# Spacing out the side work of the experts' stages in a two-block transformer forward pass

## The chip, the cores and the metric

The kernel runs on one core of a Trainium2 chip. The metric is the device time of one execution in microseconds, the median of several runs. Five engines work side by side: TensorE (PE, its weight loads shown as PEld), VectorE (DVE), ScalarE (ACT), GpSimd (POOL) and SyncE (SP), which here only issues DMAs. Each takes its instructions in the order in which the program wrote them.

## What is computed

256 positions of width 2048 go through two blocks in float32. The first has four attention mixers and an MLP; the second has a retention and a recurrent branch, a cross-attention, and a layer of 16384 single-neuron experts, which the change is about:

```python
def peer_ffn(xn, w_q, sub_keys, u_tab, v_tab):
    q = (xt @ w_q).reshape(t, PEER_HEADS, 2, PEER_HALF)
    sub_scores = jnp.einsum('thcd,hckd->thck', q, sub_keys).astype(jnp.float32)
    vals, ids = lax.top_k(sub_scores, PEER_TOPK)
    cand = vals[:, :, 0, :, None] + vals[:, :, 1, None, :]
    top_sc, pos = lax.top_k(cand.reshape(t, PEER_HEADS, PEER_TOPK * PEER_TOPK), PEER_TOPK)
    i1 = jnp.take_along_axis(ids[:, :, 0], pos // PEER_TOPK, axis=-1)
    i2 = jnp.take_along_axis(ids[:, :, 1], pos % PEER_TOPK, axis=-1)
    gate = jax.nn.softmax(top_sc, axis=-1)
    ...
    act = jax.nn.gelu(jnp.einsum('td,tkd->tk', xb, u))
    return jnp.einsum('tk,tkd->td', gb * act, v_tab[eb])
```

For each position and head the 16 best of 16384 experts are selected. The kernel computes the activations of all experts, makes a dense matrix G of gates that is zero where an expert wasn't selected, and multiplies W = G x activation with the whole table v.

## The kernel before, in words

**One stream of weights.** Class Stream (line 43) holds all large matrix products of the program in one list. A piece is 1 MB of weights (128 x 2048 floats); it is loaded on SyncE's queue into a tile raw (three of them, load, line 69) and used in two half pieces of 128 x 1024. Each half piece is split into a rounded part whi (ScalarE copy, line 84) and the rest wlo (a subtraction, line 87), so that three products with rounded operands give float32 accuracy. There are five whi and five wlo tiles. Method run (line 139) goes through the half pieces in order: at half piece i it writes the split of half piece i+3 (ahead, line 90), then the products of half piece i, then the "end" of the output if this was its last half piece, and then some steps of the side work.

**Two modes.** In mode "w" the weights stand still and a half piece is 8 pairs of a 512-column product (line 173) and a 256-column product (line 174). In mode "t" the activations stand still and a half piece is 12 products of 512 columns (lines 163 to 165). Sums are in two PSUM tiles called mm, taken in turn.

**Side work** is a list of Python generators. Method steps (line 118) goes through the list once in each half piece and lets each generator write its instructions up to its next yield. A plain yield counts against the half piece's budget; "pause" and "wait" do not. The budget is 2 steps in the stage w_q and in the stage v, and 1 in the stage u (rate=1, line 1440). With even=True it is also 1, and the end of a generator doesn't count either. Nothing else sets the order: it is fixed when the program is built.

**The experts' stages** (peer, line 1390) are three runs of the stream:
- w_q, 32 half pieces, mode w: the queries. Every second half piece's wlo is made on GpSimd here (pool=2, lines 86 and 1408). Side work: normed (line 1464) scales the layer's input, two GpSimd operations for each of eight tiles fx, to give the tiles fn; topk (line 1498), once for each of four quarters of the heads, selects with top16 (line 1478: MAX8, MAX_INDEX and MATCH_REPLACE on VectorE, four rows each) and looks the numbers up with tiles eq, compared on VectorE (line 1555) and multiplied on GpSimd (line 1557).
- u, 256 half pieces, mode w: the activations, an output every four half pieces. gelu_pair (line 1445) works on each in three rounds of a ScalarE and a VectorE operation, directly in the PSUM tile, and stores the result (ad). Side work: the rest of topk, then gates (line 1564), 64 rounds with "yield" and "pause" in turn, which write G to memory (gd).
- v, 256 half pieces, mode t, 16 groups of 16. Four tiles W for each group come from weigh (line 1613): two products wx<-A,G on VectorE, a rounded copy on ScalarE (line 1635), a subtraction on VectorE (line 1636). weigh for a group runs while the group ahead of it is multiplied, after A and G came by DMA. At each output's end v_end (line 1419) adds the sums to the residual h (VectorE, line 1423, the profile's acc<-mm,acc).

After the last group finish (line 1643) does the final norm and stores the output.

The lines on which the order turns:

```python
            if j.get("even"):
                s.steps(1, ("wait", "pause", "end"))
            else:
                s.steps(j.get("rate", 2))
```

## Time and profile before

| what | value |
|---|---|
| median of 3 runs | 3544.64 us (3544.45 to 3547.34) |
| profiled execution, its own time | 3546.58 us |
| its span, first to last instruction | 3544.5 us |
| PE busy | 3483.2 us (98%) |
| PEld busy | 2957.8 us (83%) |
| DVE busy | 2306.4 us (65%) |
| ACT busy | 1636.6 us (46%) |
| POOL busy | 324.3 us (9%) |
| mean granted TensorE clock | 0.995 of full speed |
| moved by DMA | 703.84 MB, 199 GB/s |

The profile was taken on one execution. Busy is the time in which an engine had an instruction running; products overlap, each being shown at about 390 ns while the next one starts 227 ns after it, so a short wait of TensorE shows up smaller in its busy time than it is. The granted clock is 1 at full speed (2.4 GHz) and 0.5 at the lower level (1.2 GHz); for a stretch it is given as a mean.

### The profile page before, as it was taken

Reading aid. Unit: us, or ns where it says so; the run is one execution under the profiler, and the core shown is the slowest. Engines: PE = TensorE matmul, PEld = TensorE weight load, DVE = VectorE, ACT = ScalarE, POOL = GpSimd, SP = SyncE. Lnnn points to the kernel's source line nnn. Section 1 sums busy time; section 2 is a strip of 40 time slices with the busy share of each in tenths; the row PEclk is TensorE's granted clock in tenths of the full one; section 3 lists DMA queues with packets and bytes.
Section 4 is the critical chain, followed back from the end, with each engine's and each line's share of the span. In section 5 each row is a group of like instructions: output and inputs, shape, how many; then the busy total and the mean of one; then the engine's idle time right before and its main releaser. Section 6 shows DMA issues by size and latency. Waiting matters only on the chain.

```text
span 3544.5 us, 45984 instructions
## 1 busy us (share of the span) xinstructions
PE 3483.2 (98%) x18204; PEld 2957.8 (83%) x18204; DVE 2306.4 (65%) x3412; ACT 1636.6 (46%) x2298; POOL 324.3 (9%) x342
## 2 busy tenths in 40 slices
PE   9999999999999999999999899999999999999998
PEld 7788888888888888888888788888888888888887
DVE  5565565645555567875555998777776566766665
ACT  5455444444343454545444344555554444444443
POOL 0000000000000000010003522222220000000000
PEclk9999999999999999999999999999999999999999
DMA  6544455555555555445544455666666576666654
GB/s 217 173 143 164 176 184 179 200 183 196 181 197 197 206 185 196 155 157 197 204 156 169 148 196 206 220 231 208 232 220 251 201 270 235 237 237 237 238 208 154
DMA packets 112567, 703.84 MB, mean 199 GB/s; under 512 B 12708, under 2 KB 13493, under 8 KB 39392
## 3 DMA queue, kind: packets, MB, share of 16 engines
q1 hardware_dynamic: 87120, 610.98, 48.2%
q0 software_dynamic: 24944, 89.85, 7.3%
q8 instruction: 143, 2.34, 0.3%
q14 instruction: 72, 0.59, 0.0%
q10 hardware_dynamic: 288, 0.07, 0.0%
HBM read 660.98 MB, written 39.87 MB: 198 GB/s over the span
## 4 chain that ended last, share of the span: by engine, by line
PE 80%; DVE 10%; issue 6%; ACT 3%; POOL 1%; DMA 1%; ACTq 0%; POOLq 0%; SPq 0%; DVEq 0%
PE mm L173 26%; PE mm L174 13%; PE mm L164 11%; PE mm L163 11%; PE mm L165 11%; DVE wlo L87 4%; ACT whi L84 2%; DVE wx L1632 2%; PE ss L1602 2%; PE ss L318 1%; PE ss L266 1%; PE ss L345 1%; DVE eq L1555 0%; PE ss L1381 0%; PE ss L1359 0%
## 5 line engine op out<-in xcount | busy, mean ns | idle before, releaser
L87 DVE TENSOR_TENSOR wlo<-raw,whi 128x1024 fp32r<-128x1024 f32 (+2 forms) x1146 | 1394.8, 1240 | 460.2 <-ACT whi L84 458.6
L84 ACT ACTIVATE whi<-raw 128x1024 fp32r<-128x1024 f32 (+2 forms) x1162 | 1187.2, 1049 | 451.9 <-PE mm L165 330.1
L173 PE MATMUL mm<-xT,whi 128*128 128x512 f32 x2368 | 847.7, 401 | 0.0
L173 PE MATMUL mm<-fn,whi 128*128 128x512 f32 x2048 | 731.9, 401 | 3.6 <-ACT whi L84 2.6
L174 PE MATMUL mm<-xT,wlo 128*128 128x256 f32 x2368 | 666.2, 281 | 9.3 <-DVE wlo L87 9.1
L174 PE MATMUL mm<-fn,wlo 128*128 128x256 f32 x2048 | 576.5, 281 | 10.1 <-DVE wlo L87 10.1
L173 PEld LDWEIGHTS mm<-xT,whi 128*128 128x128 f32 x2368 | 446.6, 189 | 107.4 <-issue 1.6
L173 PEld LDWEIGHTS mm<-fn,whi 128*128 128x128 f32 x2048 | 387.8, 189 | 93.2 <-ACT whi L84 2.9
L174 PEld LDWEIGHTS mm<-xT,wlo 128*128 128x128 f32 x2368 | 449.1, 190 | 13.1 <-DVE wlo L87 12.3
L164 PE MATMUL mm<-wlo,W 128*128 128x512 f32 x1024 | 400.3, 391 | 12.2 <-DVE wlo L87 12.2
L174 PEld LDWEIGHTS mm<-fn,wlo 128*128 128x128 f32 x2048 | 390.1, 190 | 12.5 <-DVE wlo L87 12.5
L163 PE MATMUL mm<-whi,W 128*128 128x512 f32 x1024 | 399.5, 390 | 0.0
L165 PE MATMUL mm<-whi,W 128*128 128x512 f32 x1024 | 398.5, 389 | 0.0
L164 PEld LDWEIGHTS mm<-wlo,W 128*128 128x128 f32 x1024 | 192.2, 188 | 56.6 <-DVE wlo L87 17.2
L163 PEld LDWEIGHTS mm<-whi,W 128*128 128x128 f32 x1024 | 192.2, 188 | 43.2 <-ACT whi L84 3.4
L165 PEld LDWEIGHTS mm<-whi,W 128*128 128x128 f32 x1024 | 192.2, 188 | 39.5
L163 PE MATMUL mm<-whi,hid 128*128 128x512 f32 x512 | 199.8, 390 | 0.0
L165 PE MATMUL mm<-whi,hid 128*128 128x512 f32 x512 | 199.3, 389 | 0.0
L164 PE MATMUL mm<-wlo,hid 128*128 128x512 f32 x512 | 199.3, 389 | 0.0
L1423 DVE TENSOR_TENSOR acc<-mm,acc 128x512 f32<-128x512 f32 x128 | 82.2, 683 | 104.6 <-PE mm L165 104.6
L1452 DVE TENSOR_TENSOR mm<-mm,act 128x512 f32<-128x512 f32 x64 | 44.7, 698 | 153.3 <-ACT act L1451 153.3
L1451 ACT ACTIVATE act<-mm 128x512 f32<-128x512 f32 x64 | 38.2, 597 | 228.6 <-PE mm L174 228.6
(507 smaller groups left out, 4166.8 us busy)
## 6 DMA issues: line engine op xcount, KB each, us to landing
raw<-in_peer_u SPq DMA_DIRECT2D x128, 1024.0 KB, 5.0
raw<-in_peer_v SPq DMA_DIRECT2D x128, 1024.0 KB, 5.0
raw<-in_w_up SPq DMA_DIRECT2D x64, 1024.0 KB, 5.1
raw<-in_w_down SPq DMA_DIRECT2D x64, 1024.0 KB, 4.9
raw<-in_w_in_w SPq DMA_DIRECT2D x52, 1024.0 KB, 4.9
raw<-in_w_out SPq DMA_DIRECT2D x32, 1024.0 KB, 5.0
raw<-in_w_in_t SPq DMA_DIRECT2D x22, 1024.0 KB, 4.8
raw<-in_w_xv SPq DMA_DIRECT2D x16, 1024.0 KB, 4.9
```

Source lines behind the costliest of these rows:

```text
L84: s.nc.scalar.activation(hi[:, :w], raw, AF.Copy)
L87: e.tensor_tensor(lo[:, :w], raw, hi[:, :w].bitcast(F32), op=ALU.subtract)
L163: nc.tensor.matmul(o, xh, w, start=st, stop=False, skip_group_check=True)
L164: nc.tensor.matmul(o, xh, v, start=False, stop=False, skip_group_check=True)
L165: nc.tensor.matmul(o, xl, w, start=False, stop=en, skip_group_check=True)
L173: nc.tensor.matmul(o, w[:, c], xt[:, :, kl], start=st, stop=False, skip_group_check=True)
L174: nc.tensor.matmul(o[:, 0], v[:, c], xt[:, 0, kl], start=False, stop=en, skip_group_check=True)
L1423: nc.vector.tensor_tensor(h[:, m], acc[m], h[:, m], op=ALU.add)
L1451: nc.scalar.activation(a, z, AF.Copy)
L1452: nc.vector.tensor_tensor(y, y, a, op=ALU.add)
L1602: nc.tensor.matmul(p[:, j * 128:(j + 1) * 128], o[0][:, j], o[1][:, j], start=True, stop=True)
L1632: nc.vector.tensor_tensor(x[:, :, 128 * i:128 * i + 128], a[:, 2 * (e % 2):2 * (e % 2) + 2, 128 * i:128 * i + 128], G[s][i].rearrange("p ( ...
```

## The change

- **steps** knows a new word: a generator that yields "rest" ends the side work of this half piece, also for those behind it in the list.
- **Budgets**: w_q, u and v all get even=True, so one counting step in each half piece.
- **Selection and gates**: topk, top16 and gates yield "rest" after most of their steps, so such a step is written only in every second half piece; normed too.
- **No GpSimd** for the wlo of w_q, for fx in normed and for the product on eq in topk: all are VectorE's now. GpSimd keeps the product on oh in gates, a conversion in topk, and its DMAs.
- **gelu_pair** begins a half piece later and works on a tile ux in SBUF in place of the PSUM tile.
- **v_end** writes the additions a half piece later, except for the last output.
- **weigh** makes W in three stages over six half pieces: in one half piece the products of tile e, the rounded copy of tile e-1 and the subtraction of tile e-2. After the first load of A and G it lets four half pieces go by.

```diff
@@ Stream.steps
-            n -= s.step(g) not in idle
+            r = s.step(g)
+            if r == "rest":
+                return
+            n -= r not in idle
@@ peer: w_q, v_end, v, u
-                  pool=2,
+                  even=True,
...
         def v_end(s, n):
-            def end(acc):
+            def add(acc):
+                if (s, n) != (15, 3):
+                    yield "pause"
                 h = self.h[n]
                 for m in range(2):
                     nc.vector.tensor_tensor(h[:, m], acc[m], h[:, m], op=ALU.add)
+                if s == 15:
+                    S.side.append(self.finish(n))
+
+            def end(acc):
+                S.spawn(add(acc), first=True)
                 if n == 3:
                     have.add(f"v{s}")
-                if s == 15:
-                    S.side.append(self.finish(n))
...
-                      end=v_end(s, n))
+                      end=v_end(s, n), even=True)
...
-                  end=u_end(u), need=lambda kbs: kbs[-1] // 2 in self.fn, rate=1,
+                  end=u_end(u), need=lambda kbs: kbs[-1] // 2 in self.fn, even=True,
@@ gelu_pair
-        a = self.half_act[c][:, 2 * u:2 * u + 2]
+        a, x = self.half_act[c][:, 2 * u:2 * u + 2], self.w([128, 2, 256], "ux")
+        yield "pause"
         nc.scalar.activation(a, z, AF.Copy)
-        nc.vector.tensor_tensor(y, y, a, op=ALU.add)
+        nc.vector.tensor_tensor(x, y, a, op=ALU.add)
...
@@ normed
-            nc.gpsimd.tensor_tensor(x, t[:, 0].bitcast(F32), t[:, 1].bitcast(F32), op=ALU.add)
-            nc.gpsimd.tensor_tensor(x, x, self.Rf[:, None, :].to_broadcast([128, 2, 256]), op=ALU.mult)
-            yield "pause"
+            nc.vector.tensor_tensor(x, t[:, 0].bitcast(F32), t[:, 1].bitcast(F32), op=ALU.add)
+            nc.vector.tensor_tensor(x, x, self.Rf[:, None, :].to_broadcast([128, 2, 256]), op=ALU.mult)
+            yield "rest"
@@ top16
             if i:
                 yield
+                yield "rest"
             for v, idx, s in rows:
                 nc.vector.max_index(idx[:, c], v[:, c], s)
             yield
+            yield "rest"
@@ topk
         nc.vector.tensor_tensor(b, qs[:, 2], t[:, 0], op=ALU.subtract)
         yield
+        yield "rest"
...
-                    nc.gpsimd.tensor_tensor(eq[m][:, h], eq[m][:, h],
+                    nc.vector.tensor_tensor(eq[m][:, h], eq[m][:, h],
@@ gates
             yield
-            yield "pause"
+            yield "rest"
@@ weigh
         load(0)
+        for _ in range(4):
+            yield "pause"
         for s in range(16):
...
-            for e in range(4):
-                t, x = self.xe("W"), self.w([128, 2, 256], "wx")
...
-                nc.scalar.activation(t[:, 0], x, AF.Copy)
-                nc.vector.tensor_sub(t[:, 1], x, t[:, 0].bitcast(F32))
-                self.W[s, e] = t
+            W, X = {}, {}
+            for e in range(6):
+                if e > 1:
+                    nc.vector.tensor_sub(W[e - 2][:, 1], X[e - 2], W[e - 2][:, 0].bitcast(F32))
+                    self.W[s, e - 2] = W[e - 2]
+                if 0 < e < 5:
+                    W[e - 1] = self.xe("W")
+                    nc.scalar.activation(W[e - 1][:, 0], X[e - 1], AF.Copy)
+                if e < 4:
+                    X[e] = x = self.w([128, 2, 256], "wx")
...
                 yield
+            del G[s], A[s]
```

How it moves the instructions, at three places of VectorE's order. Rows with L87 are the splits, one for each half piece; what stands between two of them is what one half piece's side work adds (the line numbers of the change are up to 20 higher).

**First place: the selection, in w_q before.** tv and cv are the values found, ti and ci their places, sub and cand what is searched.

```order
L87 TENSOR_TENSOR wlo<-raw,whi 128x1024
L1485 MAX tv<-sub 128x8 x4
L1489 MAX_INDEX ti<-tv,sub 128x8 x4
L1474 TENSOR_TENSOR fn<-fx,fn 128x512
L1493 MATCH_REPLACE sub<-tv,sub 128x128 x4
L1485 MAX tv<-sub 128x8 x4
L87 TENSOR_TENSOR wlo<-raw,whi 128x1024
L1489 MAX_INDEX ti<-tv,sub 128x8 x4
L405 SCALAR_TENSOR_TENSOR pq<-mm,pq 128x512
L1474 TENSOR_TENSOR fn<-fx,fn 128x512
```

The same kind of steps with the change (a later quarter, in u; ux and act belong to gelu_pair):

```order
L1494 MAX cv<-cand 128x8 x4
L1499 MAX_INDEX ci<-cv,cand 128x8 x4
L87 TENSOR_TENSOR wlo<-raw,whi 128x1024 x2
L1461 TENSOR_TENSOR ux<-mm,act 128x512
L1504 MATCH_REPLACE cand<-cv,cand 128x64 x4
L1494 MAX cv<-cand 128x8 x4
L87 TENSOR_TENSOR wlo<-raw,whi 128x1024
L1464 SCALAR_TENSOR_TENSOR act<-act,ux 128x512
L87 TENSOR_TENSOR wlo<-raw,whi 128x1024
L1467 SCALAR_TENSOR_TENSOR act<-act,ux 128x512
L1499 MAX_INDEX ci<-cv,cand 128x8 x4
L87 TENSOR_TENSOR wlo<-raw,whi 128x1024 x2
```

Before, the steps of two generators and those of normed stand between two splits, and every second split is missing from this engine; with the change each split is here, and a step of the selection is followed by a half piece without one.

**Second place: the end of the selection**, before:

```order
L87 TENSOR_TENSOR wlo<-raw,whi 128x1024
L1555 TENSOR_TENSOR eq<-qs,cst 128x256 x4
L1561 TENSOR_REDUCE i_129<-eq 128x32 x2
L1555 TENSOR_TENSOR eq<-qs,cst 128x256 x4
L1485 MAX tv<-sub 128x8 x4
L1489 MAX_INDEX ti<-tv,sub 128x8 x4
L87 TENSOR_TENSOR wlo<-raw,whi 128x1024
```

and with the change (L1569 is the product that was GpSimd's):

```order
L87 TENSOR_TENSOR wlo<-raw,whi 128x1024
L1567 TENSOR_TENSOR eq<-qs,cst 128x256
L1569 TENSOR_TENSOR eq<-eq,tf 128x256
L1567 TENSOR_TENSOR eq<-qs,cst 128x256
L1569 TENSOR_TENSOR eq<-eq,tf 128x256
L1567 TENSOR_TENSOR eq<-qs,cst 128x256
L1569 TENSOR_TENSOR eq<-eq,tf 128x256
L1567 TENSOR_TENSOR eq<-qs,cst 128x256
L1569 TENSOR_TENSOR eq<-eq,tf 128x256
L87 TENSOR_TENSOR wlo<-raw,whi 128x1024
L1461 TENSOR_TENSOR ux<-mm,act 128x512
L1573 TENSOR_REDUCE i_129<-eq 128x32 x2
```

Four comparisons became four comparisons and four products; the next such group stands in the half piece right behind.

**Third place: a group's W in the stage v**, before:

```order
L1423 TENSOR_TENSOR acc<-mm,acc 128x512 x2
L1632 TENSOR_TENSOR wx<-A,G 128x2x128 x2
L1636 TENSOR_TENSOR W<-wx,W 128x512
L87 TENSOR_TENSOR wlo<-raw,whi 128x1024
L1632 TENSOR_TENSOR wx<-A,G 128x2x128 x2
L1636 TENSOR_TENSOR W<-wx,W 128x512
L87 TENSOR_TENSOR wlo<-raw,whi 128x1024
L1632 TENSOR_TENSOR wx<-A,G 128x2x128 x2
L1636 TENSOR_TENSOR W<-wx,W 128x512
L87 TENSOR_TENSOR wlo<-raw,whi 128x1024
L1632 TENSOR_TENSOR wx<-A,G 128x2x128 x2
```

and with the change:

```order
L1654 TENSOR_TENSOR wx<-A,G 128x2x128 x2
L87 TENSOR_TENSOR wlo<-raw,whi 128x1024
L1428 TENSOR_TENSOR acc<-mm,acc 128x512 x2
L1654 TENSOR_TENSOR wx<-A,G 128x2x128 x2
L87 TENSOR_TENSOR wlo<-raw,whi 128x1024
L1645 TENSOR_TENSOR W<-wx,W 128x512
L1654 TENSOR_TENSOR wx<-A,G 128x2x128 x2
L87 TENSOR_TENSOR wlo<-raw,whi 128x1024
L1645 TENSOR_TENSOR W<-wx,W 128x512
L1654 TENSOR_TENSOR wx<-A,G 128x2x128 x2
L87 TENSOR_TENSOR wlo<-raw,whi 128x1024
L1645 TENSOR_TENSOR W<-wx,W 128x512
```

Before, each subtraction into W stands right behind its own products; with the change it stands two half pieces behind them, and there is one tile's work in a half piece. In the whole order the last comparison for gates stands at VectorE's split 864 of 1162 (before at 839 of 1146, with 16 more splits on GpSimd, so at half piece 9 earlier), and the first half piece of v is that of split 910.

## Rows read from the trace of the kernel before

**Rows 1.** Busy time by stretch: start:end, length, PE, PEld, DVE, ACT, POOL, PEclk, DMA, GB/s.

```profile
1900.00:2150.00 250.00, 232.60 (x1288) 200.46 (x1287) 216.99 (x643) 106.98 (x140) 109.97 (x78) 0.97 0.50 177
...
2650.00:2750.00 100.00, 95.92 (x536) 82.69 (x536) 62.84 (x72) 48.56 (x67) 10.84 (x16) 0.97 0.68 244
...
2818.00:3532.00 714.00, 701.84 (x3071) 574.76 (x3070) 491.67 (x568) 296.35 (x328) 31.18 (x59) 1.00 0.63 226
...
1950.00:2000.00 50.00, 43.20 (x239) 37.25 (x237) 47.78 (x151) 18.73 (x24) 39.22 (x27) 0.93 0.43 152
```

**Rows 2.** What TensorE waited for, in 1900:2150 and in 2818:3532: us, times, longest.

```profile
PE mm L174 <- DVE wlo L87: 15.8, 8, 3.7
...
PE mm L164 <- DVE wlo L87: 12.2, 16, 0.8
```

**Rows 3.** Timeline around 1967 us: start, duration, instruction, [idle before it <- releaser].

```profile
1965.27 0.40 PE L173 MATMUL mm<-xT,whi 128*128 128x512 f32 x1
...
1967.39 0.39 PE L173 MATMUL mm<-xT,whi 128*128 128x512 f32 x1
1971.45 0.58 PE L174 MATMUL mm<-xT,wlo 128*128 128x256 f32 x1 [3.66 <-DVE wlo L87]
...
1967.55 3.85 DVE L87 TENSOR_TENSOR wlo<-raw,whi 128x1024 fp32r<-128x1024 f32 x1
...
1973.99 1.20 DVE L87 TENSOR_TENSOR wlo<-raw,whi 128x1024 fp32r<-128x1024 f32 x1
...
1966.71 2.38 POOL L87 TENSOR_TENSOR wlo<-raw,whi 128x1024 fp32r<-128x1024 f32 x1
```

**Rows 4.** One line's instructions each: duration in ns, min/median/max.

```profile
L87 DVE TENSOR_TENSOR wlo<-raw,whi x1146: 557/1222/3848, 9.3 to 3524.8; 128x1024 fp32r<-128x1024 f32 x188, 128x640 fp32r<-128x640 f32 x2, 128x384 fp32r<-128x384 f32 x1
...
L1555 DVE TENSOR_TENSOR eq<-qs,cst x32: 407/421/2009, 1982.6 to 2130.8; 128x256 f32<-128x256 f32 x32
...
L1557 POOL TENSOR_TENSOR eq<-eq,tf x32: 725/913/2586, 1983.0 to 2132.3; 128x256 f32<-128x256 f32 x32
```

**Rows 5.** VectorE's timeline, one step of the selection, and the reduction of eq.

```profile
1991.03 0.86 DVE L1485 MAX8 tv<-sub 128x8 f32<-128x128 f32 x4
...
1992.86 2.93 DVE L87 TENSOR_TENSOR wlo<-raw,whi 128x1024 fp32r<-128x1024 f32 x1
1995.72 1.27 DVE L1561 TENSOR_REDUCE i<-eq 128x32 f32<-128x512 f32 x2
1996.90 0.08 DVE L1493 MATCH_VALUE_LOAD sub<-tv,sub 128x8 f32 x1
...
1997.95 0.86 DVE L1485 MAX8 tv<-sub 128x8 f32<-128x128 f32 x4
```

**Rows 6.** Timeline of the stage v over one making of W: VectorE, then TensorE.

```profile
2957.30 1.23 DVE L87 TENSOR_TENSOR wlo<-raw,whi 128x1024 fp32r<-128x1024 f32 x1 [0.26 <-ACT whi L84]
2958.44 1.19 DVE L1632 TENSOR_TENSOR wx<-A,G 128x256 f32<-128x256 f32 x2
2960.33 0.69 DVE L1636 TENSOR_TENSOR W<-wx,W 128x512 fp32r<-128x512 f32 x1 [0.70 <-ACT W L1635]
2961.28 1.23 DVE L87 TENSOR_TENSOR wlo<-raw,whi 128x1024 fp32r<-128x1024 f32 x1 [0.26 <-ACT whi L84]
...
2960.07 0.39 PE L164 MATMUL mm<-wlo,W 128*128 128x512 f32 x1
...
2968.91 0.39 PE L164 MATMUL mm<-wlo,W 128*128 128x512 f32 x1
...
2970.57 0.50 PE L164 MATMUL mm<-wlo,W 128*128 128x512 f32 x1 [0.76 <-DVE wlo L87]
```

**Rows 7.** Timeline of VectorE: the first products of weigh.

```profile
2692.07 0.69 DVE L1632 TENSOR_TENSOR wx<-A,G 128x256 f32<-128x256 f32 x1 [4.68 <-DMA G<-gd]
```

**Rows 8.** What ScalarE and VectorE waited for in 2818:3532: us, times, longest.

```profile
ACT whi L84 <- DMA raw<-in_peer_v: 62.2, 20, 4.8
...
DVE acc L1423 <- PE mm L165: 98.1, 32, 3.1
```

More of the change, by code (lines that the diff above doesn't have):

```diff
@@ L1449, in gelu_pair @@
             self.half_act[c] = self.g([128, 4, 256], "act")
-        a = self.half_act[c][:, 2 * u:2 * u + 2]
+        a, x = self.half_act[c][:, 2 * u:2 * u + 2], self.w([128, 2, 256], "ux")
+        yield "pause"
         nc.scalar.activation(a, z, AF.Copy)
-        nc.vector.tensor_tensor(y, y, a, op=ALU.add)
+        nc.vector.tensor_tensor(x, y, a, op=ALU.add)
         yield "pause"
-        nc.scalar.activation(a, y, AF.Square, scale=0.044715 ** 0.5)
-        nc.vector.scalar_tensor_tensor(a, a, 1.0, y, op0=ALU.add, op1=ALU.mult)
+        nc.scalar.activation(a, x, AF.Square, scale=0.044715 ** 0.5)
+        nc.vector.scalar_tensor_tensor(a, a, 1.0, x, op0=ALU.add, op1=ALU.mult)
         yield "pause"
         nc.scalar.activation(a, a, AF.Tanh, scale=(2.0 / np.pi) ** 0.5)
-        nc.vector.scalar_tensor_tensor(a, a, 1.0, y, op0=ALU.add, op1=ALU.mult)
+        nc.vector.scalar_tensor_tensor(a, a, 1.0, x, op0=ALU.add, op1=ALU.mult)
         if u == 1:
@@ L1627, in weigh @@
                 yield from self.wait(f"v{s - 2}" if s > 1 else "u")
-            for e in range(4):
-                t, x = self.xe("W"), self.w([128, 2, 256], "wx")
-                a = A[s][e // 2].rearrange("p (b t) -> p b t", b=4)
-                for i in range(2):
-                    nc.vector.tensor_tensor(x[:, :, 128 * i:128 * i + 128],
-                                            a[:, 2 * (e % 2):2 * (e % 2) + 2, 128 * i:128 * i + 128],
-                                            G[s][i].rearrange("p (t i) -> p i t", i=8)[:, 2 * e:2 * e + 2], op=ALU.mult)
-                nc.scalar.activation(t[:, 0], x, AF.Copy)
-                nc.vector.tensor_sub(t[:, 1], x, t[:, 0].bitcast(F32))
-                self.W[s, e] = t
+            W, X = {}, {}
[8 more added lines that the diff above has]
+                    X[e] = x = self.w([128, 2, 256], "wx")
+                    a = A[s][e // 2].rearrange("p (b t) -> p b t", b=4)
+                    for i in range(2):
+                        nc.vector.tensor_tensor(x[:, :, 128 * i:128 * i + 128],
+                                                a[:, 2 * (e % 2):2 * (e % 2) + 2, 128 * i:128 * i + 128],
+                                                G[s][i].rearrange("p (t i) -> p i t", i=8)[:, 2 * e:2 * e + 2], op=ALU.mult)
                 yield
+            del G[s], A[s]
             if s + 1 < 16:
```

## The prediction

> **What bounds the kernel now.** The table of engines shows TensorE at 98% of the span; no other engine is near. So time can only be won where TensorE waits or runs at its lower clock, and I read in this order: busy time by stretch (where), what TensorE waited for (on whom), and the timelines there (why). By stretch [rows 1], three places of the experts' stages stand out.
>
> First, 1900 to 2150 us (w_q and the beginning of u): TensorE is busy 232.6 of 250 us, so idle 17.4, and its mean granted clock is 0.97. At half speed half of the time is lost, so a mean of 0.97 costs (1 - 0.97) x 250 = 7.5 us: 24.9 in all. Of that idle time 15.8 us are waits for wlo from VectorE [rows 2], which from 1950 to 2000 is busy 47.78 of 50 us [rows 1].
>
> Second, 2650 to 2750 us: 4.1 us idle and 3.0 us of clock, 7.1 in all.
>
> Third, the stage v, 2818 to 3532 us: its busy time hides waits, so I count products. Between two rows of the timeline 39 products start, in 2968.91 - 2960.07 = 8.84 us, one each 0.2267 us [rows 6]. The stage has 3071 of them [rows 1], 696.2 us at that pace; it takes 714, so 17.8 us are lost. The waits are 16, one in each group, for wlo [rows 2].
>
> The sum that can be won is 24.9 + 7.1 + 17.8 = 49.8 us.
>
> **Why TensorE waits there.** A half piece lasts 8 pairs of products in mode w: six pairs take 1967.39 - 1965.27 = 2.12 us [rows 3], so 2.8 us; in mode t 12 x 0.2267 = 2.7. Splits are written three ahead and there are five tiles, so a split's tile comes free when TensorE starts the half piece four ahead of its own. From there 4 x 2.8 = 11.2 us are left, less the subtraction's 1.22 [rows 4] and ScalarE's copy ahead of it, which I take as no longer: a **reserve of about 8.8 us**, 8.5 in v. Whatever VectorE does between two splits beyond what fits beside TensorE eats it.
>
> In w_q two things eat it. Between two of VectorE's splits stand up to two steps of topk and one of normed. And operations are drawn out while GpSimd runs: the subtraction at 1967.55 takes 3.85 us, beside one of GpSimd's that takes 2.38, while an undisturbed one takes 1.20 [rows 3].
>
> In v the four tiles W are made in two half pieces, and VectorE and ScalarE wait for each other at each: from one split to the next 2961.28 - 2957.30 = 3.98 us pass [rows 6], with idle 0.70 for ScalarE's W. Four rounds are 16 us where TensorE needs 5.4: 10.5 late against a reserve of 8.5.
>
> At 2692 us VectorE waits 4.68 us for G by DMA [rows 7], everything behind it too.
>
> **The change part by part.**
>
> *Work that moves to VectorE.* 16 subtractions at 1.22 [rows 4] are 19.5 us. 16 operations on fx, 128x512, I take at the 0.69 of the same shape [rows 6]: 11 us. 32 products on eq: VectorE doesn't do them before; the nearest row is the comparison on the same tile, 0.42 undisturbed, and above it GpSimd's own 0.91 [rows 4]: 13.4 to 29 us, I take 13.4 because it is the same engine and shape. That is 44 us. Against it, what GpSimd drew out goes: GpSimd is busy 110 us in the first stretch [rows 1], and what is left of it there is little.
>
> *Spacing.* A step of the selection is at most MAX8 and the search, 1992.86 - 1991.03 = 1.83 us, or the replacement and MAX8, 1.05 + 0.86 = 1.91 [rows 5]. In two half pieces of 5.6 us VectorE now has two subtractions (2.44), one such step (1.9) and gelu's share (three operations of the 0.69 shape [rows 6] in four half pieces, so 1.0): 5.4. That fits, barely, and draws nothing from the reserve. The exception is the selection's end, where two half pieces follow each other without rest: twice 8 x 0.42 for eq, a pair of reductions at 1.27 [rows 5], 2.44 and 1.4 for gelu make 11.8 us in 5.6, so 6.2 late, and 0.5 more in the next. The reserve of 8.8 covers it with 2 to spare. At 0.91 for a product it is 3.9 us more and TensorE waits about 2, four times; with a fall of the clock like the one above (7.5 us for the whole first stretch, which holds several) I bound this at 5 us each. So the residue lies between 0 and 20 us. I take 3, near the end that the row of the same engine gives.
>
> *The other side of spacing.* The selection ends later, at about a third of u, and gates with it. The order shows gates' last comparison at split 864 and v's first half piece at split 910: 9 half pieces later than before, over 40 half pieces or 110 us in hand. No cost.
>
> *Four half pieces of pause in weigh* are 11 us, and VectorE waited 4.68 for G [rows 7]; the wait goes, with it the 7.1 us of the second place. Behind the pause only other side work stands, of which there is none by then except gelu.
>
> *W in three stages.* In six half pieces (16.3 us) VectorE has six subtractions, four pairs of products at 1.19, four subtractions at 0.69 [rows 6] and a pair of additions, two of the 0.69 shape less some overlap, 1.3: 7.3 + 4.8 + 2.8 + 1.3 = 16.2. It fits, and no engine waits for the other, since ScalarE's copy was written a half piece before. All 17.8 us go. A and G for the next group are asked for four half pieces later; ten half pieces, 27 us, are left for them. No cost.
>
> *Additions and gelu a half piece later.* VectorE waited 98.1 us for TensorE's last product at these additions [rows 8]; part of that goes. It was no time of TensorE's, so I count nothing; the tile mm is needed again four half pieces after its output's end, which covers the delay.
>
> **The sum**: 49.8 - 3 = 46.8 us off the profiled execution's 3546.58 gives 3499.8. The median of the runs is 1.94 us below that execution, so **3498 us**. If all goes and some that I can't see (the first stretch also counts idle time too small) it is 3490; with the residue at 20 it is 3515.
>
> **A rule against it.** VectorE is at 47.78 of 50 us in the first stretch while GpSimd is idle most of the program [rows 1], and the change loads VectorE. The Trainium skill (Perfetto Trace Analysis, Optimizing Scalar/DVE Operations) says that with a saturated VectorE it may make sense to hand some work to ScalarE or even GpSimd, though it warns that the two share a read port. By the first half of that sentence the first stretch isn't won, which is the first rival; the 3.85 us in [rows 3] speak for the second half.
>
> **The rivals.**
> 1. *VectorE stays the bound of the selection.* For it: 5.4 of 5.6 us is hardly a margin, and any operation slower than I took it tips it. Against it: the load of the drawn-out operations goes. The first stretch's 24.9 us stay, the rest is won: 3544.6 - 24.9 = 3519.7, so 3520. Chance 0.13.
> 2. *Another wait takes v's place.* ScalarE waits 62.2 us in v for the weights themselves [rows 8]; if it is these that are late and not VectorE, v stays at 714: 3498 + 17.8 = 3516. Against it: TensorE's waits all name wlo, with VectorE late by W. Chance 0.07.
> 3. *Slower: the PSUM tiles.* Sums are read a half piece later and there are two tiles. If VectorE reaches the additions more than three half pieces (8.2 us) after the output's end, TensorE waits at each of the 64 outputs of v. At (46.8 + 7)/64 = 0.84 us beyond that point the whole is slower; at 1.5 us it is 3498 + 96 = 3594. Against it: VectorE waits for TensorE there, 98.1 us, and not the reverse [rows 8]. Chance 0.03.
>
> **How the numbers follow.** The forecast, 3490 to 3515, has 0.73; rivals 0.13, 0.07 and 0.03; 0.04 is for what I don't see, half of it no change, the rest equally faster and slower. The likeliest time is 3498; the range of 8 in 10 takes in both milder rivals: 3490 to 3520. A measurement tells 0.2%, 7 us, from no change. Faster: 0.73 + 0.13 + 0.07 + 0.01 = 0.94; same 0.02; slower 0.04.
>
> **What would show it.** In the profile after: no subtraction wlo near 3.85 us in w_q; TensorE idle by 3 us or less from 1900 to 2150 with the clock at 1.00; no wait for wlo in v and a stage of some 697 us; no wait of wx for G. A wait of TensorE for wlo right behind the products on eq shows the residue, or, if spread over the whole selection, the first rival. I am wrong if v still takes over 710 us or if VectorE stays full through the selection and TensorE waits for it.

## The result, and the profile after

| | before | with the change |
|---|---|---|
| median | 3544.77 us of 4 runs (3544.45 to 3547.34) | 3493.68 us of 4 runs (3492.21 to 3496.78) |
| profiled execution, its own time | 3546.58 us | 3493.89 us |
| its span | 3544.5 us | 3492.1 us |
| from the span's start to u's first product | 2018.5 us | 2001.5 us |
| u, to v's first product | 799.3 us | 782.0 us |
| v, first to last product | 714.3 us | 696.1 us |
| what follows | 12.4 us | 12.4 us |

The change makes the kernel faster: ratio 0.9856, 95% interval 0.9844 to 0.9868, 51.1 us less by the medians and 52.4 by the spans. The forecast was 3498 us, its range 3490 to 3520. By the lower rows of the table 17.0 us went ahead of u's first product, 17.3 in u and 18.2 in v. The 17.0 are not all w_q's: w_q's own first product comes at 1910.3 us before and at 1908.5 with the change, so 1.8 of them lie ahead of it.

The page of the changed kernel, its span and its table of engines:

```profile
span 3492.1 us, 46015 instructions
...
PE 3463.2 (99%) x18204; PEld 2950.4 (84%) x18204; DVE 2295.6 (66%) x3476; ACT 1655.1 (47%) x2298; POOL 232.5 (7%) x278
```

Busy time by stretch (columns as in [rows 1]). The first three rows are the stretches that stand there too, the fourth is v where it now lies:

```profile
1900.00:2150.00 250.00, 250.00 (x1438) 218.46 (x1437) 206.83 (x522) 123.93 (x156) 15.10 (x14) 1.00 0.59 202
1950.00:2000.00 50.00, 50.00 (x293) 43.82 (x292) 36.60 (x87) 22.06 (x27) 0.00 (x0) 1.00 0.52 182
2650.00:2750.00 100.00, 100.00 (x579) 87.16 (x578) 67.29 (x76) 54.42 (x73) 10.07 (x16) 1.00 0.74 264
2784.00:3480.00 696.00, 696.00 (x3071) 576.01 (x3069) 487.04 (x565) 303.72 (x327) 31.18 (x59) 1.00 0.66 232
```

TensorE is busy in every microsecond of the three places that lost time, at a granted clock of 1.00, and v does the same 3071 products in 696 us that took 714. What TensorE waited for from 1900 to 3480 us is one row, where [rows 2] had 24 waits for wlo:

```profile
PE ss L1614 <- POOL oh L1600: 1.4, 1, 1.4
```

One making of W in v, VectorE's timeline, the counterpart of [rows 6]. Between two splits 2.87 us pass, where it was 3.98, and W stands behind no wait for ScalarE:

```profile
2916.63 1.23 DVE L87 TENSOR_TENSOR wlo<-raw,whi 128x1024 fp32r<-128x1024 f32 x1
2917.76 0.70 DVE L1645 TENSOR_TENSOR W<-wx,W 128x512 fp32r<-128x512 f32 x1
2918.37 1.24 DVE L1654 TENSOR_TENSOR wx<-A,G 128x256 f32<-128x256 f32 x2
2919.50 1.25 DVE L87 TENSOR_TENSOR wlo<-raw,whi 128x1024 fp32r<-128x1024 f32 x1
```

The operations that the prediction had to price, one line's instructions each (ns, minimum/median/maximum):

```profile
L1569 DVE TENSOR_TENSOR eq<-eq,tf x32: 424/425/426, 2033.7 to 2246.3; 128x256 f32<-128x256 f32 x32
...
L1479 DVE TENSOR_TENSOR fx<-xT x8: 682/684/686, 1923.5 to 1962.6; 128x512 f32<-128x512 f32 x8
```

So the size of the gain was foreseen. The experiments ask which part of the change made it, and there the prediction's reasons did less well.

### The profile page after: what moved, and what is told of

The parts are those of the page before. It is cut to its first block, busy times and chain, and to the rows that moved or that the text cites. A ratio compares the mean times of both kernels' runs of the same rounds, so it can differ in the third digit from the quotient of the medians.

```text
span 3492.1 us, 46015 instructions
## 1 busy us (share of the span) xinstructions
PE 3463.2 (99%) x18204; PEld 2950.4 (84%) x18204; DVE 2295.6 (66%) x3476; ACT 1655.1 (47%) x2298; POOL 232.5 (7%) x278
## 4 chain that ended last, share of the span: by engine, by line
PE 92%; issue 4%; DVE 3%; ACT 1%; DMA 0%; POOL 0%; SPq 0%; POOLq 0%; DVEq 0%; ACTq 0%
PE mm L176 30%; PE mm L177 15%; PE mm L166 13%; PE mm L168 13%; PE mm L167 13%; PE ss L1614 2%; DVE wlo L87 1%; PE ss L321 1%; PE ss L269 1%; PE ss L348 1%; PE ss L1362 0%; PE ss L1384 0%; PE ss L333 0%; ACT whi L84 0%; PE ss L796 0%
## 5 line engine op out<-in xcount | busy, mean ns | idle before, releaser
L87 DVE TENSOR_TENSOR wlo<-raw,whi 128x1024 fp32r<-128x1024 f32 (+2 forms) x1162 | 1394.7, 1217 | 676.1 <-ACT whi L84 675.0
L1616 ACT ACTIVATE gst<-ss 128x256 f32<-128x256 f32 x128 | 42.3, 383 | 174.2 <-PE ss L1614 174.2
L168 PEld LDWEIGHTS mm<-whi,hid 128*128 128x128 f32 x512 | 96.1, 188 | 20.1
L166 PEld LDWEIGHTS mm<-whi,hid 128*128 128x128 f32 x512 | 96.1, 188 | 19.8
```

Source lines behind the costliest of these rows:

```text
L87: e.tensor_tensor(lo[:, :w], raw, hi[:, :w].bitcast(F32), op=ALU.subtract)
L166: nc.tensor.matmul(o, xh, w, start=st, stop=False, skip_group_check=True)
L168: nc.tensor.matmul(o, xl, w, start=False, stop=en, skip_group_check=True)
L1616: nc.scalar.activation(st[i][:, :, 4 * a:4 * a + 4].rearrange("p g t i -> p t g i"), p.rearrange("p (t a g i) -> p a t g i", t=4, a=2, i=8 ...
```

## The experiments

Times below are medians. Each kernel's program ahead of 1850 us is that of the change, but executions differ: u's first product comes at 2001.3 to 2008.3 us in kernels in which nothing ahead of it was touched.

So a few microseconds are not read from totals, but from waits or from the stretch between two products. All of that difference lies ahead of w_q's first product (1908.3 to 1915.3 us). From there to the start of u's 217th half piece it is 761.94 to 762.00 us in the changed kernel and in all those that change nothing there; this stretch, called **the selection's stretch** below, holds the first place and all of gates. In the last 40 half pieces behind it the pace differs: they take 113.07 us in the changed kernel and three others, and 110.93 in three in which TensorE waits for nothing there either. So spans can differ by 2 us for this alone; the reason was not looked for.

The kernel before was timed anew in each group, at 3544.48, 3543.21 and 3545.91 us, and the ratios are to these.

### First group: the stage v, and the pause in weigh

The first three vary W's stages and the budget of steps in v:

```diff
# one stage: for each tile, within one half piece
-            for e in range(6):
+            for e in range(4):
...
+                nc.scalar.activation(t[:, 0], x, AF.Copy)
+                nc.vector.tensor_sub(t[:, 1], x, t[:, 0].bitcast(F32))
+                self.W[s, e] = t
                 yield
# two steps: in v
-                      end=v_end(s, n), even=True)
+                      end=v_end(s, n), even=2)
...
-                s.steps(1, ("wait", "pause", "end"))
+                s.steps(int(j["even"]), ("wait", "pause", "end"))
```

> The change, but each tile W is made in one step again (products, ScalarE's copy, subtraction behind each other), still one step in a half piece. Theory (VectorE's reserve of 8.5 us decides): a round takes 3.98 us as before, beside 2.72 us of TensorE, so four rounds run 5 us late, 6.3 with the additions; that is under 8.5, TensorE waits for nothing in v: about 3494 us, v in 697 us. Rival (the mutual waits of VectorE and ScalarE make TensorE wait, whatever the reserve): the 17.8 us come back, 3512 us, v in 714.

> The change, but with two counting steps in a half piece in v, so W's six steps take three half pieces. Theory of the reserve: VectorE has 3 x 1.22 + 4 x 1.19 + 4 x 0.69 + 1.3 = 12.5 us there, TensorE 8.2; 4.3 late is under 8.5: 3494 us, v in 697. Rival (it is the density of steps that costs): waits in each group again, up to 3512 us.

> The change, but W in one stage and two counting steps in v, as before the change: four rounds of 3.98 us in two half pieces, 10.5 late against 8.5. Both theories: the stage v has its waits again, 1.1 us in each of 16 groups, 712 to 715 us for v and 3510 to 3513 us in all.

Measured: 3495.95, 3495.82 and 3495.90 us (ratios to the kernel before 0.9864, 0.9861 and 0.9863, intervals about 0.0017 to each side), and v takes 696.1 us in all three. The third is a clear miss, and it showed a misreading: weigh is one generator, steps goes through the list once in a half piece, so a budget of two never gives it two steps. The two-step kernels have the same order of instructions as their one-step counterparts, so they are repeats. And W in one stage does not bring back a microsecond in v. In that kernel VectorE still stays for ScalarE (0.70) in each round and takes 4.0 us from split to split (the last two rows), as before:

```profile
2911.80 1.20 DVE L1646 TENSOR_TENSOR wx<-A,G 128x256 f32<-128x256 f32 x2
...
2915.80 1.28 DVE L1428 TENSOR_TENSOR acc<-mm,acc 128x512 f32<-128x512 f32 x2
2916.99 1.19 DVE L1646 TENSOR_TENSOR wx<-A,G 128x256 f32<-128x256 f32 x2
2918.89 0.69 DVE L1650 TENSOR_TENSOR W<-wx,W 128x512 fp32r<-128x512 f32 x1 [0.70 <-ACT W L1649]
2919.84 1.23 DVE L87 TENSOR_TENSOR wlo<-raw,whi 128x1024 fp32r<-128x1024 f32 x1 [0.26 <-ACT whi L84]
...
2923.84 1.23 DVE L87 TENSOR_TENSOR wlo<-raw,whi 128x1024 fp32r<-128x1024 f32 x1 [0.26 <-ACT whi L84]
```

But the first round (2911.80) came a half piece ahead of the additions (2915.80), and these find the sums ready: there is no idle time in their row.

The fourth kernel takes the pause out:

```diff
         load(0)
-        for _ in range(4):
-            yield "pause"
         for s in range(16):
```

> The change without the four half pieces of pause behind the first load of A and G. Theory: with the pauses VectorE still waited 3.3 us for G, so without them it waits 3.3 + 11.2 = 14.5 us, 5.7 more than the reserve of 8.8; TensorE waits 5 to 6 us and its clock falls once: 3494 + 7 to 9, so 3501 to 3503 us. Rival (the 7.1 us of that place came from W's mutual waits, which are gone now): 3494 us.

Measured: 3497.66 us (3495.79 to 3501.09), ratio 0.9866 [0.9849, 0.9882], less than expected. VectorE's two waits for G are below, first without the pause, then the one that is left with it. TensorE lost 0.8 us by it.

```profile
2686.84 0.68 DVE L1652 TENSOR_TENSOR wx<-A,G 128x256 f32<-128x256 f32 x1 [6.83 <-DMA G<-gd]
...
2689.36 0.66 DVE L1652 TENSOR_TENSOR wx<-A,G 128x256 f32<-128x256 f32 x1 [1.84 <-DMA G<-gd]
```

```profile
2689.34 0.69 DVE L1654 TENSOR_TENSOR wx<-A,G 128x256 f32<-128x256 f32 x1 [3.35 <-DMA G<-gd]
```

6.83 + 1.84 = 8.7 us is about the whole reserve of 8.8, and so it was nearly hidden. The pause lets four half pieces, 11 us, go by and saves only 5.3 us of waiting: the second G landed 10.1 us after its issue without it (2679.29 to 2689.36) and 16.0 us with it (2673.37 to 2689.34). Why it then takes longer was not tried.

### Second group: what cured v, and what cured the selection

The new theory for v: before, the additions stood directly behind their output's last half piece, so VectorE was held until TensorE's last product (98.1 us in [rows 8]) and began its four rounds of 3.98 us only then. The additions end 1.3 us after that product; the splits behind the rounds are done 5.3, 9.3, 13.2 and 17.2 us after it, and TensorE needs them after 8.2, 10.9, 13.6 and 16.3, so the last is 0.9 late, once in a group. Either a shorter round or an earlier start would do. Two kernels put the additions back:

```diff
             def add(acc):
-                if (s, n) != (15, 3):
-                    yield "pause"
+                yield from ()
```

the first with W in three stages, the second with W in one (edit above).

> The change with the additions of v at the output's end again, as before the change; W stays in three stages. Theory 1 (either part alone is enough: with the additions at once VectorE comes to its first round of a group 1.3 us behind TensorE's last product, and rounds without a stay for ScalarE take 3.1 us and not 3.98, so the splits behind them are done 3.7, 6.8, 9.9 and 13.1 us after that product, needed 8.2, 10.9, 13.6 and 16.3 after it): v stays at 696 us, no wait for wlo in it, 3494 to 3497 in all. Theory 2 (the later additions alone cured v): 16 waits for wlo of 0.6 to 1.0 us, v 710 to 714 us, 3508 to 3512 in all.

> The change with the additions of v at once and W in one stage, so v in the order it had before the change. Theory 1 (either part alone is enough, the absence of both is what costs): four rounds of 3.98 us behind additions that end 1.3 us after TensorE's last product put the fourth split 0.9 us late, once in each of 16 groups: v 711 to 714 us, 3509 to 3512 in all. Theory 3 (v was cured by neither, but by the budget of one step, the deletion of G and A or something else in the change): v stays at 696 us, 3494 to 3497 in all.

Measured: 3493.88 us (3493.46 to 3494.13), ratio 0.9861 [0.9844, 0.9877], and 3511.61 us (3508.85 to 3518.91), ratio 0.9916 [0.9900, 0.9933]. v takes 696.1 and 711.9 us. Theory 1 holds in both, and the first is as fast as the change; none of the twelve was faster. What TensorE waited for in v in the second:

```profile
PE mm L167 <- DVE wlo L87: 10.7, 14, 0.8
```

14 waits, one each 44.65 us, which is a group. By the start of the product behind, each costs 0.99 us, 13.8 in all, and the next product starts 0.11 us late once more, 1.6 in all: 15.4 of the 15.8 us that v takes longer. VectorE's timeline of that kernel around one of them:

```profile
2917.40 1.29 DVE L1427 TENSOR_TENSOR acc<-mm,acc 128x512 f32<-128x512 f32 x2 [3.12 <-PE mm L168]
2918.61 1.20 DVE L1645 TENSOR_TENSOR wx<-A,G 128x256 f32<-128x256 f32 x2
2920.50 0.69 DVE L1649 TENSOR_TENSOR W<-wx,W 128x512 fp32r<-128x512 f32 x1 [0.70 <-ACT W L1648]
2921.45 1.23 DVE L87 TENSOR_TENSOR wlo<-raw,whi 128x1024 fp32r<-128x1024 f32 x1 [0.26 <-ACT whi L84]
...
2933.45 1.23 DVE L87 TENSOR_TENSOR wlo<-raw,whi 128x1024 fp32r<-128x1024 f32 x1 [0.26 <-ACT whi L84]
```

and of TensorE:

```profile
2934.73 0.50 PE L167 MATMUL mm<-wlo,W 128*128 128x512 f32 x1 [0.76 <-DVE wlo L87]
```

VectorE sits 3.12 us at the additions, then four rounds begin at 2918.61; the fourth split ends at 2933.45 + 1.23 = 2934.68, and TensorE's product starts 0.05 us later. This is the picture of [rows 6].

The other two kernels take the two causes of the first place apart. One gives GpSimd its share back and keeps the spacing:

```diff
-                  even=True,
+                  even=True, pool=2,
...
-            nc.vector.tensor_tensor(x, t[:, 0].bitcast(F32), t[:, 1].bitcast(F32), op=ALU.add)
-            nc.vector.tensor_tensor(x, x, self.Rf[:, None, :].to_broadcast([128, 2, 256]), op=ALU.mult)
+            nc.gpsimd.tensor_tensor(x, t[:, 0].bitcast(F32), t[:, 1].bitcast(F32), op=ALU.add)
+            nc.gpsimd.tensor_tensor(x, x, self.Rf[:, None, :].to_broadcast([128, 2, 256]), op=ALU.mult)
...
-                    nc.vector.tensor_tensor(eq[m][:, h], eq[m][:, h],
+                    nc.gpsimd.tensor_tensor(eq[m][:, h], eq[m][:, h],
```

> The change with GpSimd's share as before it (every second wlo of w_q, fx, the products on eq), the spacing kept. If GpSimd's drawing out of VectorE's operations was the main cause of the waits from 1900 to 2150 us: single subtractions of 3 to 4 us on VectorE beside GpSimd's of 2.4, TensorE waits 8 us or more there and the clock falls again, 3505 to 3519 in all. If the missing spacing was the main cause: TensorE loses 3 us or less there, 3494 to 3498 in all.

The other keeps everything on VectorE and takes out the spacing (in w_q and u no even, in topk, top16, gates and normed no rest, as before the change):

```diff
-                  even=True,
...
-                  end=u_end(u), need=lambda kbs: kbs[-1] // 2 in self.fn, even=True,
+                  end=u_end(u), need=lambda kbs: kbs[-1] // 2 in self.fn, rate=1,
...
-            yield "rest"
+            yield "pause"
```

> The change without its spacing in w_q and u (no rest, budgets as before), with all of VectorE's new work kept on VectorE. If the missing spacing was the main cause of the waits from 1900 to 2150 us: VectorE, with two steps of the selection, fx and a split in a half piece of 2.8 us, is late by more than its reserve; TensorE waits 15 to 30 us and the clock falls, 3509 to 3530 in all. If GpSimd was the main cause: 5 us or less, 3494 to 3500 in all.

Measured: 3499.78 us (3498.00 to 3508.38), ratio 0.9884 [0.9867, 0.9900], and 3521.61 us (3518.98 to 3524.70), ratio 0.9939 [0.9922, 0.9956]. What TensorE waited for from 1900 to 2150 us, with GpSimd's share back:

```profile
PE ss L1521 <- DMA sk<-in_sub_keys: 3.0, 1, 3.0
PE mm L177 <- POOL wlo L87: 0.7, 2, 0.4
...
PE mm L177 <- DVE wlo L87: 0.3, 1, 0.3
```

and without spacing:

```profile
PE mm L177 <- DVE wlo L87: 19.2, 12, 3.3
PE ss L1518 <- DVE pq L408: 1.4, 1, 1.4
```

The selection's stretch takes 761.98 us with the change, 767.03 with GpSimd's share back (5.1 more) and 787.60 without spacing (25.6 more). So the missing spacing was the main cause: without it VectorE is late though nothing is drawn out. And without it, it matters little whose work it is: this kernel, with all on VectorE, loses 25.6 us, the kernel before, with GpSimd's share, lost 24.9 by the prediction's count. GpSimd's share alone came out between the two answers, with waits of 4 us and not 3 or less, and a time 2 us above that answer's range. In this timeline of VectorE, then TensorE, 7.33 us lie between two splits where TensorE uses one each 2.8 us; eq, the values and the search of the next set follow one another without a rest:

```profile
1986.53 1.22 DVE L87 TENSOR_TENSOR wlo<-raw,whi 128x1024 fp32r<-128x1024 f32 x1
1987.67 1.27 DVE L1569 TENSOR_REDUCE i<-eq 128x32 f32<-128x512 f32 x2
...
1992.04 0.86 DVE L1493 MAX8 tv<-sub 128x8 f32<-128x128 f32 x4
...
1993.86 1.21 DVE L87 TENSOR_TENSOR wlo<-raw,whi 128x1024 fp32r<-128x1024 f32 x1
```

```profile
1995.12 0.39 PE L177 MATMUL mm<-xT,wlo 128*128 128x256 f32 x1 [3.34 <-DVE wlo L87]
```

GpSimd does draw VectorE out, but spaced work bears it. With its share back, a subtraction into fn takes 2.21 us beside GpSimd's operations, where the undisturbed one takes 0.68, and TensorE's waits for wlo are 1.0 us in all. VectorE, then GpSimd, in that kernel:

```profile
1968.06 2.21 DVE L1483 TENSOR_TENSOR fn<-fx,fn 128x512 fp32r<-128x512 f32 x1 [1.85 <-ACT fn L1482]
1970.19 2.31 DVE L87 TENSOR_TENSOR wlo<-raw,whi 128x1024 fp32r<-128x1024 f32 x1
```

```profile
1967.32 2.40 POOL L87 TENSOR_TENSOR wlo<-raw,whi 128x1024 fp32r<-128x1024 f32 x1
1969.68 1.74 POOL L1479 TENSOR_TENSOR fx<-xT 128x512 f32<-128x512 f32 x1
```

Its largest cost is another: GpSimd's queue also issues the load of sub_keys for the next quarter, and it now stands behind eight products on eq:

```profile
2111.20 4.23 POOL L1569 TENSOR_TENSOR eq<-eq,tf 128x256 f32<-128x256 f32 x4 [0.65 <-issue]
2115.39 1.15 POOL L1513 DMA_DIRECT2D sk<-in_sub_keys  x2
```

With the change the same load is issued at 2100.89, right behind an earlier store, and no one waits for it.

### Third group: the end of u, gelu, and the reserve

Three kernels for the second place and for gelu: no pause and W in one stage (edits above); gelu's first round at its output's end; and all three.

```diff
         a, x = self.half_act[c][:, 2 * u:2 * u + 2], self.w([128, 2, 256], "ux")
-        yield "pause"
         nc.scalar.activation(a, z, AF.Copy)
```

> The change without the four half pieces of pause in weigh and with W in one stage; gelu and the additions stay a half piece later. Theory 1 (the 7 us at 2700 us were the wait for G, about 8.7 us of VectorE's time, plus the stays for ScalarE of a one-stage W, 4 x 0.9 us, against a reserve of 8.8): both together give TensorE a wait of 3 to 4 us and a fall of its clock there, 3499 to 3503 in all, where either alone cost 2 us or less. Theory 2 (it was gelu, which held ScalarE until TensorE's last product): no wait of more than 2 us there, 3494 to 3498 in all.

> The change with gelu's first round in the half piece in which its output ends, as before the change; all else as in the change. Theory 1 (the half piece's delay of gelu is worth nothing by itself, since VectorE and ScalarE stand within their reserve in u once a half): 3493 to 3497 in all, u at 782 us, no new wait of TensorE over 1 us. Theory 2 (ScalarE, held by gelu until TensorE's last product, delays the whi behind it, and VectorE, at 46 of 50 us in the selection, can't make up for it): TensorE waits 4 us or more between 2000 and 2260 us, 3498 to 3510 in all.

> The change with three things undone that touch the end of u: no pause in weigh, W in one stage, gelu at once; the additions stay a half piece later and so v stays at 696 us. All theories: the 7 us at 2650 to 2750 us come back, as a wait of TensorE of 3 to 4 us for wlo or whi and a fall of its clock, 3499 to 3504 in all. If they don't, something else in the change cured that place (gates ending later, or the spacing's order of DMAs), and the time is 3494 to 3498.

Measured: 3503.10 us (3500.40 to 3504.22), ratio 0.9879 [0.9862, 0.9895]; 3505.13 us (3497.53 to 3506.29), ratio 0.9877 [0.9861, 0.9894]; 3514.54 us (3509.56 to 3519.68), ratio 0.9915 [0.9898, 0.9931]. The stretch from 2650 to 2750 us in the kernel before is in [rows 1]; here it is without pause and with one stage, with gelu at once alone, and with all three (each row from its own kernel):

```profile
2650.00:2750.00 100.00, 94.23 (x541) 81.25 (x540) 63.98 (x73) 52.21 (x70) 9.53 (x15) 1.00 0.72 251
```

```profile
2650.00:2750.00 100.00, 100.00 (x592) 88.47 (x591) 67.85 (x78) 53.22 (x74) 14.98 (x20) 1.00 0.76 272
```

```profile
2650.00:2750.00 100.00, 95.64 (x535) 82.39 (x534) 62.73 (x73) 49.44 (x68) 11.03 (x16) 0.97 0.71 248
```

All three undone, the stretch is that of before: 95.64 busy at 0.97, where it was 95.92 at 0.97. Its 7 us had two causes of VectorE's lateness together, the wait for G and the stays of W's rounds. No pause alone lost TensorE 0.8 us there, one stage alone 1.5, both 5.8, and not the 3 to 4 that were expected; the clock, expected to fall, fell only when gelu was at once too. That both cost more than the sum fits a reserve: what fits into it costs nothing. The total with all three is above what was expected, for two reasons: gelu costs in the selection too, as follows, and v takes 698.5 us, with two waits for wlo of 0.75 us in its first group, where the kernel before had two as well.

Gelu at once does nothing there, but it costs elsewhere, against theory 1. What TensorE waited for from 2000 to 2300 us:

```profile
PE ss L1613 <- POOL oh L1599: 6.0, 1, 6.0
PE mm L177 <- DVE wlo L87: 2.9, 2, 1.5
PE ss L1586 <- DVE i L1572: 1.6, 1, 1.6
```

and VectorE from 2000 to 2260 us, in that kernel and then in the changed one:

```profile
DVE ux L1460 <- ACT act L1459: 21.2, 13, 2.6
```

```profile
DVE ux L1461 <- ACT act L1460: 7.8, 8, 1.3
```

VectorE, which has little time to spare in the selection, waited 13.4 us more for gelu's copy on ScalarE, which itself waits for TensorE's last product, and only 7.8 us less elsewhere. The selection ends later, two splits and the numbers i are late: 4.5 us of TensorE's waits, as theory 2 had it. The 6.0 us for oh are something else. With gelu at once alone, the first product on oh on GpSimd took 5.50 us; in the kernel with all three undone, whose order is the same up to there, it took 1.35 and TensorE waited 0.7. The durations of all 64, in the first and in the second kernel:

```profile
L1599 POOL TENSOR_TENSOR oh<-oh,gtr x64: 1029/1356/5495, 2264.4 to 2667.3; 128x512 f32<-128x512 f32 x64
```

```profile
L1599 POOL TENSOR_TENSOR oh<-oh,gtr x64: 1057/1356/1422, 2262.5 to 2659.0; 128x512 f32<-128x512 f32 x64
```

In the first, VectorE's operations follow one another without a break from the start of that product, at 2264.36, to 2268.96, none of them longer than usual, and GpSimd ends 0.9 us after the last: here GpSimd is drawn out and not VectorE. The selection's stretch takes 773.27 us in the first kernel, 11.3 more than with the change, and 767.34 in the second, 5.4 more. So the half piece's delay of gelu is worth about 5 us, and 11 when that product is held. Whether this also explains that the first kernel's four runs lie at 3497.53 and three times near 3505.5 is not shown: only one execution, of 3505.13 us, was traced.

The last kernel measures the reserve. Each comparison of eq is made four times:

```diff
-                    nc.vector.tensor_tensor(eq[m][:, h], pl[:, 2 * m + h, :, None].to_broadcast([128, 16, 16]),
+                    for _ in range(4):
+                        nc.vector.tensor_tensor(eq[m][:, h], pl[:, 2 * m + h, :, None].to_broadcast([128, 16, 16]),
```

> The change with each comparison of eq made four times, same result: 24 more VectorE instructions of 0.42 us, which follow one another every 0.33 us, in two half pieces without rest, 8 us more, at the end of each of the four selections. If the working of the prediction holds (6.2 to 6.7 us late there, a reserve of 8.8, so 2 to spare): TensorE waits some 6 us at each of four places, and its clock falls behind each, 3518 to 3530 in all. If there is more to spare than that: waits of 0 to 3 us each, 3494 to 3508 in all.

Measured: 3535.20 us (3532.90 to 3540.32), ratio 0.9968 [0.9956, 0.9981], later than both theories said. Four comparisons on one tile take 1.80 us, one 0.42, so a repeat costs 0.46 and not 0.33, and the 24 at one place 11.0 us. TensorE's waits from 2000 to 2320 us:

```profile
PE mm L177 <- DVE wlo L87: 22.2, 3, 7.7
PE ss L1588 <- DVE i L1574: 9.3, 1, 9.3
```

Three waits for wlo of 7.4 us on average, for 11.0 us more work: 3.6 us were to spare. The prediction had worked out 2. The fourth selection has no split behind which to hide: there TensorE waits 9.3 us for the numbers themselves.

## Why the prediction was right, and where it was not

**What bounds the kernel, and the sum: right.** The three places were all that was lost, and all of it went: 24.9, 7.1 and 17.8 us were seen to be lost, 49.8 in all, and the span fell by 52.4. Of the 2.6 us more, 1.8 lie ahead of w_q's first product, where executions differ anyway, and are no gain of the change; from there to v's first product the gain is 32.4 for 32.0, in v 18.2 for 17.8. The clock had cost a little more than was worked out: the mean of 0.97 stood for 17.1 us at the lower level (1.2 GHz) in the first place, half of them lost, 8.5 us and not 7.5. One reading was wrong without consequence: the 16 waits in v are not one in each group, but two in the first and none in the last, in which no W is made.

**The residue of 3 us: 0.** No split is late at the selection's ends; what is left is a wait of 1.4 us for oh, which the sum did not have. The prices held: 0.425 for the product on eq (taken 0.42), 0.684 for fx (0.69). The spare of 2 us measured 3.6.

**Why VectorE was late in the selection: half right.** The prediction named too much work between two splits and GpSimd's drawing out, and did not weigh them. Spacing carries it: without it the selection's stretch is 25.6 us longer, of which 19.2 + 1.4 us are waits in the first place. GpSimd's share back costs 5.1 us, and only 1.0 of it is wait for wlo; the wait of 3.0 for sub_keys was not among the prediction's steps, which should have asked what GpSimd's queue issues behind its products. What was set against the change, the suggestion of the Trainium skill (Perfetto Trace Analysis, Optimizing Scalar/DVE Operations) to hand work of a saturated VectorE to GpSimd, did not pay here: the same work back on GpSimd made the time longer. The Trainium skill's own caution beside it, that VectorE and GpSimd share a read port and such a move might not help, is the half that held; the 2.21 us against 0.68 fit it.

**"Four tiles W are made in two half pieces", and W in three stages: the step that failed.** A tile takes a half piece, so four rounds are 16 us against 10.9, not 5.4. The lateness of the rounds alone, 5.1, is within the reserve. What made it too much was that the rounds began behind the additions, which waited for TensorE's last product: so VectorE was a half piece and the additions, 2.7 + 1.3 us, late before the first round. Three stages are one cure and the additions' delay the other; each alone gives 696.1 us, without both it is 711.9. The number, 17.8, was right because the place was emptied whichever way.

**"Additions and gelu a half piece later ... I count nothing": the other step that failed.** VectorE's 98.1 us at the additions were called no time of TensorE's. They were not, but they set when VectorE could begin the work behind, and that was TensorE's. The additions' delay is worth nothing beside three stages and 16 us without them; gelu's is worth 5 to 11 us in the selection.

**"The wait goes" (weigh's pause): wrong, without consequence.** 3.35 us of wait for G are left, of 6.8 in two waits, the longer being that of 4.68 [rows 7]. The pause alone is worth about 1 us of TensorE's time; the 7.1 us went because W's rounds became shorter as well.

**The rivals.** VectorE is still near full in the selection (43.7 to 46.6 us of each 50 from 2000 to 2250 us), but no split is late, so the first fell. v is at 696.1, so weights were not what was late: the second fell. TensorE waits nowhere for a PSUM tile: the third fell.

## What to carry to other kernels

An in-order engine that waits for the bottleneck's newest result gives away its lead, and whatever is queued behind starts that much later: where much work stands behind such an instruction, write it a step later, even where its own wait costs nothing by the profile. Side work beside a saturated engine is best spread so that each step fits into the time of the step it hides behind; a reserve hides single lapses, and two lapses in it cost more than their sum. To learn which of several edits made a gain, undo them in pairs too: edits that cure the same wait each look worthless alone.

## What the hardware showed that I had not expected

The clock did not fall with each long wait. In the kernel without spacing the wait of 3.34 us that ends at 1995.12 left the granted clock at full speed (2.4 GHz), while with three of 2.27 to 2.45 us, which end at 2034.81, 2044.63 and 2070.92, it went to the lower level for 3.4 us each, from 2034.6, 2044.8 and 2072.2 on; with GpSimd's share back the 3.0 us for sub_keys cost no clock (rows: without spacing, 1950 to 2000 and 2050 to 2100 us, then that kernel, 2100 to 2150 us). With each of the four waits of 7.0 to 9.3 us in the kernel with the comparisons made four times it did fall.

```profile
1950.00:2000.00 50.00, 41.01 (x238) 34.94 (x237) 48.68 (x170) 18.62 (x24) 2.25 (x3) 1.00 0.42 137
...
2050.00:2100.00 50.00, 47.73 (x270) 41.71 (x269) 46.47 (x130) 25.34 (x33) 1.62 (x3) 0.97 0.61 207
```

```profile
2100.00:2150.00 50.00, 47.04 (x277) 41.30 (x277) 42.15 (x106) 23.74 (x30) 11.08 (x12) 1.00 0.55 193
```

So a forecast that adds a fall of the clock to each wait is too dear, and what a single wait costs in clock stays open. And VectorE repeats an operation on one tile each 0.46 us where comparison and product in turn go on after 0.45 and 0.35: which instruction follows which changes the pace by some 0.1 us, which the rows of durations don't show. Beside GpSimd it is not always VectorE that is drawn out: fn took 2.21 us and not 0.68 in one kernel, the product on oh 5.50 and not 1.35 on GpSimd in another.
